# The planner of a diffusion step's instruction order keeps account of which engine last used each PSUM bank

## The chip, the cores and the metric

The kernel runs on one core of one Trainium2 chip. The time is the device time of one execution in microseconds; of several runs the median is given. Five engines work side by side, each through its own queue in order: TensorE (PE, with its weight loads shown as PEld), VectorE (DVE), ScalarE (ACT), GpSimd (POOL) and SyncE (SP), whose queue issues the DMAs. TensorE writes its products into PSUM, which DVE and ACT read; PSUM is used here as eight banks, `bank0` to `bank7`, each of 128 partitions by 512 float32 columns (line 492).

## The reference

One inference step of a backbone with two layers over 384 tokens (256 latent tokens, 128 context tokens) of width 1024, all in float32. Cut to what matters:

```
for l in range(2):
    sh1, sc1, gt1, sh2, sc2, gt2 = split(silu(cond) @ w_mod[l] + b_mod[l], 6)   # for each token group
    h = rmsnorm(x, g[l,0]) * (1 + sc1) + sh1
    if l == 0:      # neighbourhood attention and bidirectional retention, 8 heads each
        z = h @ w_in_even;  m = concat(attention(z), retention(z)) @ w_out_even
    else:           # bidirectional HGRN2, 8 heads of 128
        z = h @ w_in_odd;   m = (rmsnorm(scan_fw(z) + scan_bw(z)) * silu(gate)) @ w_out_odd
    x = x + gt1 * rmsnorm(m, g[l,1])
    h = rmsnorm(x, g[l,2]) * (1 + sc2) + sh2
    x = x + gt2 * rmsnorm((silu(h @ w_a) * (h @ w_u)) @ w_o, g[l,3])
```

Returned are the tokens of both groups, the keys and values of the context, and the final states of retention and HGRN2.

## The kernel before

**Tiling.** The tokens lie transposed, as eight tiles of 128 features by 384 tokens (`x`, and `hh`, `hl` for a high and a low part of the normed tokens). Weights come in chunks of eight 128 x 128 blocks: a DMA into `wr`, a rounded copy `wh` by ACT, the rest `wl = wr - wh` by DVE (`split_weights`, line 536; three buffers of each). A block product is then three matmuls of 384 columns: `wh` with `hh`, `wl` with `hh`, `wh` with `hl` (`gemm`, line 649). A gemm holds one bank for each output tile; when the last matmul of a tile is emitted, an eviction is started that reads the bank and gives it back.

**Stages.** Layer 0: input products, attention, retention, output products; norm step; feed-forward (FFN) in and out; norm step. Layer 1: input products, eight HGRN2 mixers, output products; norm step; FFN. The last FFN product has tokens as rows, and its six banks are read by `leave` (line 1047). Beside this the modulation of both layers is computed, partly by TensorE (`mod_pe`, whose result ACT copies to `mev` and TensorE sums, `mod_pe_out`, line 604) and partly by DVE (`mod_dve`, line 622, with the tile `mscr`).

**What sets the order.** The program is written as some dozens of streams, Python generators, each of which yields its instructions one after the other (a tuple is issued as one) or a condition to wait for. A list scheduler, the class `Machine`, has a clock for each engine and a cost for each instruction. For the next instruction of each stream it takes the earliest start: the engine's clock, or what `deps` returns, whichever is later. It emits the one with the least start (in steps of 1/20 us, after an added lateness), and among equal ones the one of the least priority number (lines 195 to 203). `emit` moves the clock on and notes the end. Thus the order on every engine is settled while the program is built; on the chip, semaphores hold each instruction until what it depends on is done. Nothing of the planner's times remains in the program, only its order.

`deps` looks at regions: a reader waits for the last write of an overlapping region, a writer for its last reads and writes. Ends are counted later by `LEAVE` (0.20 us for PE, 0.13 for DVE, 0.14 for ACT) and starts on PE by `ARRIVE` (0.15). A matmul of fp32 operands costs 4 columns / 2400 us a column, times 0.3 where it fills 32 partitions (lines 226 and 227); a DVE operation on 384 columns 0.06 + 384/960 = 0.46 us.

**Places where two engines are in one bank**, with no region in common or both reading:

- The norm step (class `Step`, from line 884). `chain` (line 914) takes four banks. Column sums of squares go into the first, a root follows, and its reciprocal is spread over 128 partitions by matmuls (`unspread`, line 726). `moments` (line 936) does the same for the norm after the update, and the result stands in columns 0 to 383 of `b2`. There DVE reads it for the first two or three feature tiles (`normed`, line 969: `scr<-x,bank`, then ACT writes `hh` and a float32 copy, and DVE forms `hl`); after two tiles ACT copies it to `rB`. All the while `keep_busy` (line 733) has TensorE multiply constants into columns 384 to 511 of `b2`, in groups of four matmuls (`bank<-cb,ca`). `GAPS` (line 84) says how many groups there may be in each stretch; after the last spread it is five. Each of the four matmuls shows as two rows in the profile. `update` (line 961) scales and adds the layer's output to `x`, reading the first spread from a bank too (`ka<-ka,bank` in the first step).
- The eviction before a norm step (`Post.__call__`, line 771): ACT squares the bank into a scratch tile, and then ACT or DVE scales it by the modulation's gate (`fy<-bank,mod` after the first FFN).
- `probabilities` (line 1175): DVE adds biases to the first 384 columns of a bank whose last 128 are written by a later matmul.
- `retention` (line 1234): DVE reads two halves of a bank, then TensorE writes the first half again.
- `mixer` (line 1458): ACT copies the first half of a bank while TensorE transposes into the second; ACT copies 384 columns of another while TensorE writes column sums behind them.
- `leave`: ACT squares a bank, DVE multiplies it. The early norm (`squares`, line 821): ACT takes a root of 96 columns, DVE copies them.

Of the kernel before, what the change touches and what calls it, by code (L numbers as in the profile page):

```python
# [65 lines left out]
class Op:  # L66
# [3 lines left out]
    def __init__(self, eng, call, outs, ins, cost, table=None):  # L70
        self.eng, self.call, self.cost, self.table = eng, call, cost, table
        self.outs = [region(a) for a in outs]
        self.ins = [region(a) for a in ins]
# [37 lines left out]
class Machine:  # L111
    def __init__(self):
        self.clock = {"PE": 0.0, "DVE": 0.0, "ACT": 0.0, "POOL": 0.0, "SP": 0.0, "DMA": 2.8}
        self.mem = {}
        self.streams = []
        self.table = None

    def spawn(self, gen, prio, late=0.0, margin=0.0):
        self.streams.append(Stream(gen, prio, late, margin))

    def deps(self, op):
        t = 0.0
        for name, a, b, lo, hi in op.ins:
            for r in self.mem.get(name, ()):
                if r[0] < b and a < r[1] and r[2] < hi and lo < r[3] and r[4] > t:
                    t = r[4]
        for name, a, b, lo, hi in op.outs:
            for r in self.mem.get(name, ()):
                if r[0] < b and a < r[1] and r[2] < hi and lo < r[3]:
                    if r[4] > t and op.eng != "PE":  # L130
                        t = r[4]
                    if r[5] > t:
                        t = r[5]
        return t + ARRIVE[op.eng]

    def emit(self, op):
        c = self.clock
        t = max(c[op.eng], self.deps(op))
        if op.eng == "SP":
            c["SP"] = t + 0.07  # L140
            end = c["DMA"] = max(t + 1.5, c["DMA"]) + op.cost
        else:
            cost = op.cost
            if op.table is not None and op.table != self.table:
                self.table = op.table
                cost += 1.3
            if op.eng == "PE" and t < COLD:
                cost *= 2
            end = c[op.eng] = t + cost
        end += LEAVE[op.eng]  # L150
        for name, a, b, lo, hi in op.ins:
            rs = self.mem.setdefault(name, [])
            for r in rs:
                if r[0] == a and r[1] == b and r[2] == lo and r[3] == hi:
                    r[5] = max(r[5], end)
                    break
            else:
                rs.append([a, b, lo, hi, 0.0, end])
        for name, a, b, lo, hi in op.outs:
            rs = self.mem.setdefault(name, [])  # L160
            rs[:] = [r for r in rs if not (a <= r[0] and r[1] <= b and lo <= r[2] and r[3] <= hi)]
            rs.append([a, b, lo, hi, end, 0.0])
        op.call()
# [1612 lines left out]
```

## Time and profile before

| | |
|---|---|
| time, median of 3 runs | 1123.94 us (1121.73 to 1124.01) |
| the profiled execution | 1121.99 us |
| its span, first to last instruction | 1120.2 us |
| PE busy | 1087.0 us (97%), 7048 matmuls |
| DVE busy | 807.5 us (72%), 1491 instructions |
| ACT busy | 556.5 us (50%), 1046 instructions |
| POOL busy | 130.9 us (12%) |
| mean granted TensorE clock | 0.993 |

Names in the profile are `out<-in` by the program's tiles, without buffer numbers, so every bank is `bank`. A line number is often that of a helper (L228 a matmul, L246 an ACT operation, L254 a DVE operation on two tensors), so the tiles tell more than the lines. In rows in order of time the columns are start, duration, engine, line, operation, tiles, shapes, count, and in brackets the engine's idle time before it and what ended that. Matmuls overlap and their ends are modelled, so a busy PE is not a PE at its best; the count of matmuls in a stretch tells more.

### The profile page before, as it was taken

The page shows a single profiled execution, that of the slowest core. Times are in us where ns is not written, and L with a number is a line of the kernel's source. Part 1 is how long each engine was busy: PE and PEld are TensorE (multiplying, and loading weights), DVE is VectorE, ACT ScalarE, POOL GpSimd, SP SyncE. Part 2 cuts the span into 40 slices and gives each one's busy share as a digit, 9 for nine tenths or more (in the row PEclk, how much of TensorE's full clock was granted, in tenths as well). Part 3 has the DMA queues.
Part 4 walks back from the last instruction along what each step waited for, and adds up shares of the span by engine and source line. Part 5 has one row for each costly group of instructions (what it writes and reads, how often), then busy time and mean ns, then how long its engine had stood idle before and what let it go on. Part 6 is the DMA issues. An engine that isn't in the chain of part 4 may idle for free.

```text
span 1120.2 us, 18271 instructions
## 1 busy us (share of the span) xinstructions
PE 1087.0 (97%) x7048; PEld 995.5 (89%) x7048; DVE 807.5 (72%) x1491; ACT 556.5 (50%) x1046; POOL 130.9 (12%) x139
## 2 busy tenths in 40 slices
PE   7999999999999999999999999999999999999997
PEld 5778877989999999989877988889989999998885
DVE  2599986688999998994888589996785434443234
ACT  4587654667333333323765456665676333333322
POOL 1220000000000000333015145442000000000000
PEclk9999999999999999999999999999999999999999
DMA  9966553246666767564442322222324433333331
GB/s 352 364 218 233 183 195 107 94 151 235 243 236 227 245 242 244 208 229 147 150 143 81 109 86 85 86 72 100 109 81 132 151 132 119 127 123 130 115 135 60
DMA packets 51766, 181.48 MB, mean 162 GB/s; under 512 B 8640, under 2 KB 14784, under 8 KB 45152
## 3 DMA queue, kind: packets, MB, share of 16 engines
q1 hardware_dynamic: 51616, 180.24, 45.9%
q8 instruction: 55, 0.90, 0.4%
q14 instruction: 31, 0.25, 0.1%
q0 software_dynamic: 64, 0.08, 0.0%
HBM read 175.83 MB, written 3.42 MB: 160 GB/s over the span
## 4 chain that ended last, share of the span: by engine, by line
PE 75%; DVE 14%; ACT 4%; issue 3%; DMA 3%; POOL 1%; SPq 0%; DVEq 0%; ACTq 0%; POOLq 0%
PE bank L228 74%; DVE wl L254 3%; DVE mscr L267 2%; ACT scr L246 1%; DMA gd<-mod 1%; DVE XB L254 1%; PE bank L232 1%; DVE XA L254 1%; ACT hh L246 1%; DMA mraw<-in_w_mod 1%; POOL ZW L252 1%; DVE scr L260 1%; DMA wr<-in_w_ffn_in 1%; DVE scr L254 0%; DVE T L260 0%
## 5 line engine op out<-in xcount | busy, mean ns | idle before, releaser
L228 PE MATMUL bank<-hh,wh 128*128 128x384 f32 (+1 forms) x1248 | 429.5, 344 | 0.0
L228 PE MATMUL bank<-hh,wl 128*128 128x384 f32 (+1 forms) x1248 | 424.9, 340 | 0.8 <-DVE wl L254 0.8
L228 PE MATMUL bank<-hl,wh 128*128 128x384 f32 (+1 forms) x1248 | 393.1, 345 | 0.0
L254 DVE TENSOR_TENSOR wl<-wr,wh 128x1024 fp32r<-128x1024 f32 x216 | 273.2, 1266 | 156.3 <-ACT wh L246 156.1
L246 ACT ACTIVATE wh<-wr 128x1024 fp32r<-128x1024 f32 x216 | 228.2, 1057 | 167.4 <-PE bank L228 113.8
L228 PEld LDWEIGHTS bank<-hh,wh 128*128 128x128 f32 x1248 | 237.4, 190 | 6.7 <-ACT scr L246 2.4
L228 PEld LDWEIGHTS bank<-hl,wh 128*128 128x128 f32 x1248 | 232.9, 189 | 6.2 <-issue 2.2
L228 PEld LDWEIGHTS bank<-hh,wl 128*128 128x128 f32 x1248 | 237.0, 190 | 1.3 <-DVE wl L254 1.1
L267 DVE SCALAR_TENSOR_TENSOR mscr<-mraw,msb 128x1024 bf16<-128x1024 f32 x128 | 161.1, 1258 | 3.1 <-ACT msb L246 2.0
L246 ACT ACTIVATE fs<-bank 128x384 f32<-128x384 f32 x44 | 21.0, 492 | 90.2 <-PE bank L228 90.2
L228 PE MATMUL bank<-gh,wl 128*128 128x384 f32 x176 | 59.3, 337 | 2.3 <-DVE wl L254 2.2
L228 PE MATMUL bank<-gh,wh 128*128 128x384 f32 x176 | 58.8, 334 | 0.0
L228 PE MATMUL bank<-gl,wh 128*128 128x384 f32 x176 | 58.8, 334 | 0.0
L254 DVE TENSOR_TENSOR fs<-bank,fs 128x384 f32<-128x384 f32 x44 | 24.0, 557 | 40.0 <-PE bank L228 39.8
L228 PE MATMUL bank<-wl,gh 128*128 128x512 f32 x132 | 51.5, 390 | 0.8 <-DVE wl L254 0.8
L228 PE MATMUL bank<-wh,gh 128*128 128x512 f32 x132 | 52.0, 394 | 0.0
L228 PE MATMUL bank<-wh,gl 128*128 128x512 f32 x132 | 51.4, 389 | 0.0
L246 ACT ACTIVATE gh<-fs 128x384 fp32r<-128x384 f32 x44 | 22.3, 519 | 56.1 <-DVE fs L254 56.1
L252 POOL TENSOR_TENSOR rB<-x,fy 128x384 f32<-128x384 f32 x1 | 1.0, 1017 | 382.9 <-DVE mod L254 382.9
L228 PE MATMUL bank<-wh,hh 128*128 128x512 f32 x96 | 40.9, 426 | 0.4 <-DVE wb L271 0.3
L228 PE MATMUL bank<-wh,hl 128*128 128x512 f32 x96 | 38.9, 405 | 2.2 <-DVE hl L254 2.2
L252 POOL TENSOR_TENSOR ZW<-XB,TA 128x192 f32<-128x192 f32 x48 | 36.1, 773 | 32.2 <-ACT XA L246 18.6
(265 smaller groups left out, 1453.8 us busy)
## 6 DMA issues: line engine op xcount, KB each, us to landing
mraw<-in_w_mod SPq DMA_DIRECT2D x48, 1024.0 KB, 5.5
wr<-in_w_ffn_in SPq DMA_DIRECT2D x88, 512.0 KB, 3.3
wr<-in_w_ffn_out SPq DMA_DIRECT2D x44, 512.0 KB, 3.3
wr<-in_w_in_odd SPq DMA_DIRECT2D x40, 512.0 KB, 3.2
wr<-in_w_in_even SPq DMA_DIRECT2D x28, 512.0 KB, 5.0
wr<-in_w_out_even SPq DMA_DIRECT2D x8, 512.0 KB, 3.2
wr<-in_w_out_odd SPq DMA_DIRECT2D x8, 512.0 KB, 3.2
bias<-in_bias SPq DMA_DIRECT2D x8, 384.0 KB, 4.2
```

The costliest lines, as they stand in the source:

```text
L228: return Op("PE", lambda: self.nc.tensor.matmul(out, lhsT=lhsT, rhs=rhs, start=start, stop=stop), [out], [lhsT, rhs], cost + 0.004)
L232: return Op("PE", lambda: self.nc.tensor.transpose(out, in_, ident), [out], [in_], 0.11)
L246: return Op("ACT", lambda: self.nc.scalar.activation(out, in_, func, **kw), outs, ins, 0.1 + width(in_) / 1200, table)
L252: return Op("POOL", lambda: self.nc.gpsimd.tensor_tensor(out=out, in0=a, in1=b, op=op), [out], [a, b], 0.12 + n * 0.0021)
L254: return Op("DVE", lambda: self.nc.vector.tensor_tensor(out=out, in0=a, in1=b, op=op), [out], [a, b], 0.06 + n / 960)
L260: return Op("DVE", lambda: self.nc.vector.tensor_scalar(out=out, in0=a, scalar1=s1, scalar2=s2, op0=op0, **kw), [out], ins, 0.19 + width(o ...
L267: return Op("DVE", lambda: self.nc.vector.scalar_tensor_tensor(out=out, in0=a, scalar=s, in1=b, op0=op0, op1=op1, **kw), outs, ins, 0.1 + ...
```

## The change

`Machine` gets a table `bank`: for each tile whose name begins with "bank", the last end of each engine's instructions that read or wrote it. `deps` adds a condition: an instruction that touches such a tile may not start, in the plan, before the other engines' noted ends. Costs, priorities, streams and conditions stay as they were. The instructions are the same; their order on each engine is planned anew.

```
@@ -114,6 +114,7 @@
         self.mem = {}
         self.streams = []
         self.table = None
+        self.bank = {}
 
     def spawn(self, gen, prio, late=0.0, margin=0.0):
         self.streams.append(Stream(gen, prio, late, margin))
@@ -131,6 +132,11 @@
                         t = r[4]
                     if r[5] > t:
                         t = r[5]
+
+        for name, *_ in op.ins + op.outs:
+            for eng, end in self.bank.get(name, {}).items():
+                if eng != op.eng and end > t:
+                    t = end
         return t + ARRIVE[op.eng]
 
     def emit(self, op):
@@ -148,6 +154,9 @@
                 cost *= 2
             end = c[op.eng] = t + cost
         end += LEAVE[op.eng]
+        for name, *_ in op.ins + op.outs:
+            if name.startswith("bank"):
+                self.bank.setdefault(name, {})[op.eng] = end
         for name, a, b, lo, hi in op.ins:
             rs = self.mem.setdefault(name, [])
             for r in rs:
```

More of the change, by code (lines that the diff above doesn't have):

```diff
@@ L116, in __init__ @@
         self.table = None
+        self.bank = {}
     def spawn(self, gen, prio, late=0.0, margin=0.0):
@@ L133, in deps @@
                         t = r[5]
+        for name, *_ in op.ins + op.outs:
+            for eng, end in self.bank.get(name, {}).items():
+                if eng != op.eng and end > t:
+                    t = end
         return t + ARRIVE[op.eng]
@@ L150, in emit @@
         end += LEAVE[op.eng]
+        for name, *_ in op.ins + op.outs:
+            if name.startswith("bank"):
+                self.bank.setdefault(name, {})[op.eng] = end
         for name, a, b, lo, hi in op.ins:
```

## The prediction

> **What bounds the kernel now.** I read the page first, then stretches of time, then the waits, then the order in time at the three norm steps.
>
> ```profile
> span 1120.2 us, 18271 instructions
> PE 1087.0 (97%) x7048; PEld 995.5 (89%) x7048; DVE 807.5 (72%) x1491; ACT 556.5 (50%) x1046; POOL 130.9 (12%) x139
> PE 75%; DVE 14%; ACT 4%; issue 3%; DMA 3%; POOL 1%; SPq 0%; DVEq 0%; ACTq 0%; POOLq 0%
> ```
>
> ```profile
> core 0: us, PE busy (x) PEld busy (x) DVE busy (x) ACT busy (x) POOL busy (x), PEclk, DMA share, GB/s
> 260.00:280.00 20.00, 20.00 (x116) 20.00 (x115) 15.68 (x25) 14.35 (x21) 0.00 (x0) 1.00 0.57 201
> 480.00:500.00 20.00, 17.77 (x100) 16.81 (x99) 19.79 (x30) 5.95 (x8) 6.56 (x5) 1.00 0.63 230
> ```
>
> TensorE bounds it: a saturated stretch holds 116 wide products in 20 us (0.172 us each), and no order makes that shorter. An order can only act where TensorE waits: at the norm steps, in the mixers, and where DVE is full and the weight splits come late (480 to 500 us, 16 products short). In the first norm step the waits on one bank can be read directly:
>
> ```profile
> 240.72 1.13 PE L228 MATMUL bank<-rs,cb 128*128 128x96 f32 x8 [0.55 <-DVE rs L277]
> 241.78 0.65 PE L228 MATMUL bank<-cb,ca 128*32 128x128 f32 x16
> 242.35 1.05 PE L228 MATMUL bank<-ca,mev 128*128 128x2 f32 x8
> 242.49 0.56 DVE L254 TENSOR_TENSOR scr<-x,bank 128x384 f32<-128x384 f32 x1 [0.37 <-PE bank L228]
> 243.08 0.98 ACT L246 ACTIVATE hh<-scr,mod 128x256 fp32r<-128x256 f32 x2 [1.03 <-DVE scr L254]
> 243.34 0.64 PE L228 MATMUL bank<-cb,ca 128*32 128x128 f32 x16
> 244.05 0.55 DVE L254 TENSOR_TENSOR scr<-x,bank 128x384 f32<-128x384 f32 x1 [1.00 <-PE bank L228]
> 244.52 0.55 DVE L254 TENSOR_TENSOR ka<-ka,bank 128x384 f32<-128x384 f32 x1
> 244.66 0.43 PE L228 MATMUL bank<-cb,ca 128*32 128x128 f32 x8 [0.68 <-DVE scr L254]
> 245.01 0.45 PE L228 MATMUL bank<-hh,wh 128*128 128x384 f32 x1
> 247.32 0.30 PEld L228 LDWEIGHTS bank<-hl,wh 128*128 128x128 f32 x2 [0.27 <-DVE hl L254]
> ```
>
> The row at 240.72 spreads 1/rms into columns 0 to 383 of a bank. The `cb,ca` rows are keep_busy: filler products into columns 384 to 511 of the same bank, five groups of eight rows (16, 16, 8). DVE reads the first columns at 242.49 and 244.05. No address is shared, yet DVE waits for the filler (0.37, 1.00 us) and the filler for DVE (0.68). So the program holds a whole bank for one engine at a time, and the old planner did not know it.
>
> **The change, part by part.** No instruction is added or removed. The tiles show as `bank` in the rows, so the test on the name should hit. What changes is a ready time, at the places where two engines meet in one bank without meeting in an address.
>
> *The norm steps (three).* By the planner's own costs (lines 99, 226 and 227) a filler group takes 4 x (128 x 4 / 2400 x 0.3 + 0.004) = 0.27 us, and a result of PE counts from 0.20 after its end. With the spread's end as zero, groups could start at 0, 0.27, 0.54, 0.82 and 1.09. DVE is free for its first read at about 0.44 and for the second at 0.90, and the earlier start is emitted first: two groups, read, two groups, read, one group, which is the 16, 16, 8 of the trace. Under the new rule DVE's read may start only 0.20 after the last filler group emitted, while the next group may start at that group's very end. The group always has the earlier start, and priority counts only between equal times. So I expect all five groups ahead of the first read.
>
> What that costs: two groups took 0.57 us (241.78 to 242.35), so five take 1.43. The `ca,mev` products, which the planner prices at almost nothing, stay between them and took 0.99 (242.35 to 243.34). The last product needs 0.08 to drain (0.65 against 0.57) and DVE started 0.06 later. First read: 241.78 + 1.43 + 0.99 + 0.08 + 0.06 = 244.34, that is 1.85 late. Behind it ACT's `hh` pair moves from 243.08 to 244.93 and ends at 245.91; the first wide product, at 245.01 until now because the fifth group stood before it, starts at about 246.0: 1.0 late. The second read follows at 244.8, no longer in TensorE's way, and the `ka` work of 244.52 fits ahead of the first read. The 0.27 wait for `hl` is covered. I take 0.75 us a step, between 0.5 and 1.0; below nothing would need fewer groups than five, which I see no reason for. Three steps: **+2.25**.
>
> *The TensorE clock.* Before the third step's products the clock falls, with the same filler pattern; in the second it doesn't:
>
> ```profile
> 537.35:540.76 3.41, 2.68 (x30) 2.19 (x30) 2.57 (x8) 3.13 (x7) 0.00 (x0) 1.00 0.99 418
> 827.49:830.90 3.41, 2.74 (x50) 2.05 (x40) 2.04 (x7) 2.41 (x6) 0.00 (x0) 1.00 0.02 5
> 830.90:834.32 3.42, 3.42 (x12) 3.42 (x11) 3.39 (x7) 3.42 (x8) 0.00 (x0) 0.50 0.26 80
> 828.75 0.65 PE L228 MATMUL bank<-cb,ca 128*32 128x128 f32 x16
> 830.06 0.43 PE L228 MATMUL bank<-cb,ca 128*32 128x128 f32 x8 [0.67 <-DVE scr L254]
> 830.42 0.45 PE L228 MATMUL bank<-hh,wh 128*128 128x384 f32 x1
> 831.16 0.52 PE L228 MATMUL bank<-hh,wl 128*128 128x384 f32 x1
> ```
>
> Twelve products in 3.42 us where 0.172 each would be 2.06: 1.4 lost. After the change TensorE's last filler ends near 244.2 and the wide products begin near 246.0: an idle 1.8 us in one piece instead of the 0.68 above. The fall then gets likelier in each step. I take one more such window, **+1.4** (bounds: the present one vanishes, -1.4; all three steps have one, +2.8).
>
> [...]
>
> *Evictions that two engines read.* After a squared copy by ACT, DVE scales the same bank (lines 771 on). The planner thought both could start together:
>
> ```profile
> 446.40 0.48 DVE L260 TENSOR_SCALAR fy<-bank,mod 128x256 f32<-128x256 f32 x1 [1.29 <-ACT acc L246]
> 448.46 2.05 DVE L267 SCALAR_TENSOR_TENSOR mscr<-mraw,msb 128x1024 bf16<-128x1024 f32 x1
> DVE fy L260 <- ACT scr L246: 8.9, 3, 3.4
> PEld bank L228 <- DVE wl L254: 3.6, 4, 2.0
> ```
>
> Now the hole may be filled with other DVE work. The 1.29 lies where DVE is full and TensorE later waits 3.6 for `wl`; the 8.9 come later, in stretches where DVE is not the bound. Filled or not is even: **-0.6** (bounds -3.6, and +3.6 where a long `mscr` is put ahead of a split).
>
> *Retention and mixers.* A second product into a bank that DVE still reads, transposes and column sums behind ACT's copies:
>
> ```profile
> PEld bank L228 <- DVE ro L254: 2.5, 3, 1.9
> PEld bank L228 <- DVE at L254: 1.0, 3, 0.4
> PEld bank L228 <- ACT o L246: 1.5, 4, 0.5
> PEld bank L232 <- ACT XA L246: 1.0, 4, 0.3
> ```
>
> TensorE can put wide products ahead of these. But the planner's new knowledge is one read longer (0.3 to 0.5 us), not the 1.9, which is DVE being late; and part of every wait is the change of product kind. I take **-0.4** for each pair, -0.8 (bounds -6.0 and 0).
>
> *At nothing.* In attention, DVE's first read of the scores waits for three groups of products; this cost DVE 1.8 us:
>
> ```profile
> DVE as L254 <- PE bank L228: 1.8, 3, 1.1
> DVE rsd L271 <- ACT rs L246: 2.7, 1, 2.7
> 1114.00 0.69 DVE L254 TENSOR_TENSOR x<-bank,mraw 128x512 f32<-128x512 f32 x1 [0.69 <-ACT hh L246]
> ```
>
> TensorE has other products meanwhile; without them it is at most -1.8. The early norm's 2.7 is ACT's own square root, which DVE's next step needs anyhow. At the end there is no other work to put in the 0.69, and TensorE's order is written out. But from the early norm on, times in the plan shift, and ties fall otherwise; that has no sign and is in the range. DMA starts follow the splits on SP's queue and move with them.
>
> **Sum:** 2.25 + 1.4 - 0.6 - 0.8 = +2.25, against the profiled execution's 1121.99 (span 1120.2 and 1.8 around it): 1124.2. That execution lies 1.95 under the median 1123.94; the four times known (1121.73, 1123.94, 1124.01, 1121.99) average 1122.9. Set on that average, as a new median would be: **1125.2 us**.
>
> **The rivals.** [...]
>
> *Better order wins (faster).* The place is DVE's queue between 446 and 492 us and retention: splits go ahead of readers that cannot start. Price: all 3.6 of the waits for `wl` and 2.5 of those for `ro` vanish. 2.25 - 6.1 = -3.85: 1119.1. It decides once these gains pass the three steps' 2.25 (and no window is added). For it: DVE idles 1.29 in a full stretch. Against it: the same hole can take a `mscr` of 2.05.
>
> *Worse order in the full stretch.* Exactly that: the splits get later and the 3.6 doubles; with the forecast's other terms 1125.2 + 0.6 + 3.6 = 1129.4.
>
> *Nothing moves.* The names don't match, or the filler stays between the reads: 1122.9. Against it: `bank` in every row.
>
> **How the numbers follow.** Forecast 0.34, clock holds 0.20, better order 0.24, worse order 0.14, nothing 0.08. This kernel's times can tell 0.2%, 2.2 us. Slower: forecast less 0.04 for smaller sizes, plus worse order, 0.44; faster: better order, 0.24; the rest, 0.32, is no change. Own range of the forecast, with steps of 0.5 to 1.0, one or two windows, gains of 0 to 2.8: 1123.0 to 1128.7. Both signs are open, so the full range goes from the better order to the worse one and a little beyond, for ties: 1118.5 to 1131.0.
>
> **What would show it.** Right: one row of 40 `cb,ca` products (cut only by `ca,mev`) before the first `scr<-x,bank` in each step, the two reads back to back, the first wide product about 1 us later after the spread; more windows at 0.50. Wrong: 16, 16, 8 again; the waits for `wl` between 440 and 500 gone, or doubled; a mixer stretch with other product counts per 20 us.

## The result, and the profile after

The changed kernel takes 1136.07 us (median of 4 runs, 1134.55 to 1136.97), the kernel before 1123.74 us in its four runs (1121.73 to 1124.01): a ratio of 1.0102, with a 95% interval of 1.0085 to 1.0119. It is slower by 12.3 us. The profiled execution took 1134.55 us, its span is 1132.7 us, the mean granted clock fell from 0.993 to 0.984. The page's head, the engines' busy time and the chain (helpers' line numbers lie nine higher than before):

```profile
span 1132.7 us, 18244 instructions
PE 1091.3 (96%) x7048; PEld 999.4 (88%) x7048; DVE 806.0 (71%) x1491; ACT 555.2 (49%) x1045; POOL 125.5 (11%) x139
PE 74%; DVE 15%; ACT 4%; DMA 3%; issue 3%; SPq 0%; POOL 0%; DVEq 0%; ACTq 0%; POOLq 0%
```

These lines show only that the same 7048 matmuls took longer. Where the time went is read from the starts of the same instruction in both traces, stage by stage. The table gives the time from one landmark to the next in both profiles; the differences add up to what the spans differ by:

| from one landmark of TensorE to the next | before, us | after, us | added |
|---|---|---|---|
| start to the last spread of step 1 (layer 0 with its products) | 240.72 | 249.12 | +8.40 |
| each last spread to the first wide product, three steps | 4.29, 4.35, 4.29 | 5.34, 5.34, 5.33 | +3.08 |
| first wide product of step 1 to the first product of FFN-out | 189.21 | 187.45 | -1.76 |
| from there to the last spread of step 2 | 100.82 | 101.82 | +1.00 |
| first wide product of step 2 to the last spread of step 3 (mixers) | 286.74 | 287.09 | +0.35 |
| first wide product of step 3 to the last stage (FFN) | 189.13 | 190.73 | +1.60 |
| last stage to the end | 100.62 | 100.47 | -0.15 |
| sum | | | +12.52 |

Part of the first row is work moved, not lost: 32 rows of the modulation's products (`mraw,sc`) stood in the first FFN stretch before (from 252.10 on) and stand ahead of that stretch after, which is 1.76 shorter.

**The norm step** has the order that the prediction gave. In order of time, step 1 after:

```profile
250.19 0.43 PE L237 MATMUL bank<-cb,ca 128*32 128x128 f32 x8
250.54 1.05 PE L237 MATMUL bank<-ca,mev 128*128 128x2 f32 x8
251.53 1.08 PE L237 MATMUL bank<-cb,ca 128*32 128x128 f32 x32
252.84 1.01 DVE L263 TENSOR_TENSOR scr<-x,bank 128x384 f32<-128x384 f32 x2
253.42 0.98 ACT L255 ACTIVATE hh<-scr,mod 128x256 fp32r<-128x256 f32 x2 [2.96 <-DVE scr L263]
254.46 0.69 PE L237 MATMUL bank<-hh,wh 128*128 128x384 f32 x1 [1.86 <-ACT hh L255]
```

All 40 filler rows stand ahead of DVE's first read, cut only by the `ca,mev` products; the two reads follow back to back; TensorE then has nothing for 1.86 us.

**The large loss lies in retention**, where the prediction saw at most gains. Four retention heads (pairs of heads, function `retention`) run beside layer 0's input products, and the output products need all four. The last one, before:

```profile
188.18 1.13 PE L228 MATMUL bank<-qk 64*128 64x256 f32 x8
190.15 0.48 PE L228 MATMUL bank<-qk 64*128 64x128 f32 x2
193.00 0.44 PE L228 MATMUL bank<-hl,wh 128*128 128x384 f32 x1
```

Its scores (`bank<-qk`) come at 188.18, and wide products follow it from 193.00 on. After, TensorE and one row of DVE:

```profile
197.99 1.07 PE L237 MATMUL bank<-mraw,sc 128*32 128x256 f32 x16
199.78 1.05 PE L237 MATMUL bank<-ca,mev 128*128 128x2 f32 x8 [0.72 <-ACT mev L255]
200.76 1.53 PE L237 MATMUL bank<-qk 64*128 64x256 f32 x8
202.73 1.45 PE L237 MATMUL bank<-qk 64*128 64x128 f32 x4 [0.45 <-DVE ro L263]
207.69 0.55 PE L237 MATMUL bank<-scr,cse 128*32 128x96 f32 x8 [1.17 <-ACT scr L255]
210.81 2.90 PE L237 MATMUL bank<-scr,cse 128*128 128x384 f32 x4 [2.58 <-DVE scr L263]
214.22 0.69 PE L237 MATMUL bank<-hh,wh 128*128 128x384 f32 x1 [0.51 <-ACT hh L255]
```

```profile
200.94 0.17 DVE L263 TENSOR_TENSOR mod<-bank,bmod 128x8 f32<-128x8 f32 x1 [0.53 <-PE bank L237]
```

The same scores come at 200.76, right behind products of the modulation (`mraw,sc` and `ca,mev`), and the second of them goes on only when DVE has read the modulation's bank (200.94). Between them and the `hh,wh` of 214.22 there is no product with weights at all: what follows a head (scores, weights, values, norm, `hh`) runs as one chain through three engines while TensorE waits. Stretches of time before and after, then three windows of after (columns as in the prediction's windows):

```profile
200.00:220.00 20.00, 20.00 (x109) 18.93 (x108) 12.43 (x19) 10.68 (x17) 0.00 (x0) 1.00 0.38 132
```

```profile
200.00:220.00 20.00, 15.25 (x60) 10.35 (x60) 7.55 (x18) 3.68 (x6) 0.00 (x0) 0.57 0.25 98
199.54:202.95 3.41, 2.73 (x18) 2.18 (x18) 2.23 (x7) 0.18 (x1) 0.00 (x0) 1.00 0.84 316
202.95:206.36 3.41, 3.37 (x16) 1.84 (x15) 0.97 (x4) 0.00 (x0) 0.00 (x0) 0.50 0.67 274
216.60:220.02 3.42, 3.42 (x10) 2.81 (x10) 0.64 (x2) 0.00 (x0) 0.00 (x0) 0.50 0.00 0
```

In 20 us there are 60 matmuls instead of 109. The 49 missing, at 0.172 us each, would be 8.4 us, the loss up to step 1; but this is an estimate, and that it fits so well is chance, since after was ahead when the stretch began: by the starts of their rows 672 products with weights against 633 at 200 us, then 686 against 732 at 220 us. The granted clock is 0.50 from 202.95 to 220.02, five windows; waits and clock together make it.

Why the head waits can be read in the program. A head needs two banks at once for its scores. The output products of layer 0 hold up to four, the head's result one, the norm behind retention one. The four can't be given back, because half of the output products' inputs come out of that norm, which needs all four heads. In the trace after, the modulation's next products take one too, and long before it is given back. Their rows (first and last start) in the stretch from 155 to 262 us, before and then after:

```profile
L228 PE MATMUL bank<-mraw,sc x64: 379/379/403, 235.2 to 253.7; 128*32 128x256 f32 x64
```

```profile
L237 PE MATMUL bank<-mraw,sc x64: 379/379/403, 172.1 to 248.1; 128*32 128x256 f32 x64
```

Before, this work began at 235.2, in the norm step. After, its first products run at 172.1, the next pair at 197.99, and the bank is free when DVE's read of 200.94 is done: by the program, seven banks of eight are held until then, and two are wanted. That was the theory to be tested. The rivals: that the new order in retention is bad whatever the banks are, that the modulation's work costs the time by itself, and that the loss sits in the filler.

### The profile page after: what moved, and what is told of

Same layout as the page of the kernel before. It is cut to its first block, busy times and chain, and to the rows that moved or that the text cites. A ratio compares the mean times of both kernels' runs of the same rounds, so it can differ in the third digit from the quotient of the medians.

```text
span 1132.7 us, 18244 instructions
## 1 busy us (share of the span) xinstructions
PE 1091.3 (96%) x7048; PEld 999.4 (88%) x7048; DVE 806.0 (71%) x1491; ACT 555.2 (49%) x1045; POOL 125.5 (11%) x139
## 3 DMA queue, kind: packets, MB, share of 16 engines
HBM read 175.83 MB, written 3.42 MB: 158 GB/s over the span
## 4 chain that ended last, share of the span: by engine, by line
PE 74%; DVE 15%; ACT 4%; DMA 3%; issue 3%; SPq 0%; POOL 0%; DVEq 0%; ACTq 0%; POOLq 0%
PE bank L237 73%; DVE wl L263 3%; DVE XB L263 2%; DVE XA L263 1%; DVE mscr L276 1%; DMA gd<-mod 1%; ACT scr L255 1%; ACT hh L255 1%; PE bank L241 1%; DMA mraw<-in_w_mod 1%; DVE scr L263 1%; ACT wh L255 1%; DMA wr<-in_w_ffn_in 1%; DVE scr L269 1%; DVE ZW L263 1%
## 5 line engine op out<-in xcount | busy, mean ns | idle before, releaser
L255 ACT ACTIVATE hh<-scr,mod 128x256 fp32r<-128x256 f32 (+1 forms) x64 | 31.8, 538 | 15.5 <-DVE scr L263 14.8
```

The lines of the kernel that those rows point to most:

```text
L255: return Op("ACT", lambda: self.nc.scalar.activation(out, in_, func, **kw), outs, ins, 0.1 + width(in_) / 1200, table)
```

## The experiments

Each kernel was compared with runs of the kernel before on the same chip. There are three readings for each beside its time: when the first spread of step 1 comes (before 238.04, after 246.39), how long TensorE needs from each step's last spread to its first wide product (before 4.29, 4.35, 4.29; after 5.34, 5.34, 5.33), and where the modulation's products lie.

| kernel | median us | ratio to before, 95% | first spread, step 1 | last spread to wide product |
|---|---|---|---|---|
| e1, account without the filler | 1135.31 | 1.0100 [1.0071, 1.0129] | 248.42 | 5.21, 5.90, 5.84 |
| e2, account for the filler's bank alone | 1129.31 | 1.0043 [1.0017, 1.0070] | 238.81 | 5.17, 5.18, 5.18 |
| e3, modulation later | 1124.07 | 0.9999 [0.9973, 1.0024] | 235.49 | 5.33, 5.34, 5.69 |
| e4, old rule, filler in its own bank | 1124.20 | 0.9993 [0.9962, 1.0025] | 238.06 | 3.41, 3.41, 4.05 |
| e5, output products leave two banks | 1122.93 | 0.9980 [0.9966, 0.9995] | 235.22 | 5.33, 5.34, 5.33 |
| e6, old rule, modulation early | 1127.30 | 1.0018 [1.0006, 1.0030] | 243.17 | 4.29, 4.52, 4.85 |
| e7, account from step 1 on | 1127.34 | 1.0022 [1.0009, 1.0035] | 237.85 | 5.34, 5.33, 5.84 |
| e8, e3 and own bank | 1118.58 | 0.9943 [0.9928, 0.9957] | 234.56 | 4.14, 3.42, 3.41 |
| e9, one cost changed by 0.005 us | 1121.48 | 0.9976 [0.9966, 0.9986] | 235.27 | 5.33, 5.33, 5.34 |
| e10, e5 and own bank | 1112.66 | 0.9896 [0.9878, 0.9915] | 235.42 | 3.41, 3.41, 3.41 |
| e11, e4 again, more runs | 1122.94 | 0.9990 [0.9979, 1.0001] | 236.92 | 3.41, 3.41, 3.41 |
| e12, e10 and the gate read later | 1107.36 | 0.9853 [0.9829, 0.9877] | 235.40 | 3.41, 3.41, 3.41 |

**e1: the filler outside the account.** `deps` and `emit` skip the new account for keep_busy's products.

```
-        for name, *_ in op.ins + op.outs:
+        for name, *_ in (() if op.filler else op.ins + op.outs):
...
```

> The changed kernel, but keep_busy's filler stands outside the account: it asks for no wait and notes none. If the filler put ahead of DVE's reads is what costs the norm steps about 1 us each (9.45 - 8.40, 9.68 - 8.69 and 11.07 - 10.03 us between the second spread and the first wide product), and the clock window at 254 us hangs on it, the groups show as 16, 16, 8 again and the time falls by 3 to 4.5 us against the changed kernel, to 1131.5 to 1133. The 8.3 us before the first norm step stay: the rows at the first spread near 246. If the filler is not what costs there, 1135 to 1137. If the whole loss came from the norm steps, about 1124.

Measured: 1135.31, no better than after. Step 1 in order of time:

```profile
252.22 0.43 PE L238 MATMUL bank<-cb,ca 128*32 128x128 f32 x8
252.57 1.05 PE L238 MATMUL bank<-ca,mev 128*128 128x2 f32 x8
253.56 0.43 PE L238 MATMUL bank<-cb,ca 128*32 128x128 f32 x8
254.05 0.56 DVE L264 TENSOR_TENSOR scr<-x,bank 128x384 f32<-128x384 f32 x1 [1.49 <-PE bank L238]
256.37 0.69 PE L238 MATMUL bank<-hh,wh 128*128 128x384 f32 x1
```

The old grouping (two groups, read, two groups, read, one) is back, but the `ca,mev` products, which the planner prices at almost nothing and which took 0.99 us on the chip, now fall between the first two groups. The first read comes 2.90 after the last spread (254.05 less 251.16), where it was 1.77 before. The gain expected from the grouping is eaten by one more mispriced neighbour; and the loss in retention is all there (248.42), so it has nothing to do with the filler.

**e2: the converse.** The kernel before, with the account kept only for a bank in which filler has been written, until keep_busy ends.

```
+            if op.filler:
+                self.filled.add(name)
+            if name.startswith("bank") and name in self.filled:
+                self.bank.setdefault(name, {})[op.eng] = end
...
```

> The kernel before, with the account kept only for the banks that hold filler, so only the norm steps are planned with it. By the prediction's steps (0.75 us each and one more clock window of 1.4): 1123.7 + 3.65 = 1127.4; with 1.0 us each and no window 1126.7. The attention and retention stages stay as in the kernel before (first spread near 238.0). If the delay is taken back in the feed-forward stages that follow, 1123 to 1125.

Measured: 1129.31, and each step longer by 0.88, 0.83 and 0.89 us (5.17 less 4.29, and so on). The filler part of the change alone costs about 2.6 us in the steps; the clock and the stages behind them bring the profile to +6.15.

**e3: the modulation later.** The kernel after, with the condition that lets the modulation go on moved behind layer 0's output products.

```
-        mods.allow = 10
         yield from gemm_tok(PLAN_E2, ready(0), L0.va, L0.va_in)
...
         yield from gemm(PLAN_OUT, KT, lambda k: k in L0.oh, post, keep=1)
+        mods.allow = 10
```

> The changed kernel, with one line moved: TensorE's modulation products 8 to 11 are let go only after the output products of layer 0 (as it happened in the kernel before), so that they hold no bank during retention. Theory of the bank: the last retention head waits for a bank that these products hold from 172 to 201 us while the output products hold four; then its scores come near 194 rather than 201, the five half-clock windows from 203 to 220 go, and the time falls by 6 to 9 us, to 1127 to 1130. Rival, that DVE's decays or other ties make the head late: at least 1134. Rival, that only the moved modulation products (1.7 us of TensorE) count: 1134 to 1136, as they come back later.

Measured: 1124.07, better than expected. The first spread comes at 235.49: 10.9 earlier than after, and 2.55 earlier than before. So the loss in retention goes with the modulation's early bank. No window of half clock is left between 165 and 490. With that bank out of the way, the new order of layer 0 is, in this profile, a little better than the old one. The steps still cost 5.33 and more.

**e4: a bank for the filler.** The kernel before; `chain` takes a fifth bank and keep_busy writes there and gives it back.

```
-            b, self.b, r1, self.b2 = yield from banks.take(4)
-            M.spawn(keep_busy(self.b2[:, NT:512], lambda: self.r2 is rB), 9)
+            b, self.b, r1, self.b2, fb = yield from banks.take(5)
+            M.spawn(keep_busy(fb[:, NT:512], lambda: self.r2 is rB, fb), 9)
...
```

> The kernel before, in the same order, with the filler in a fifth bank of its own, so that no read waits for it and it waits for none. If the shared bank costs real waits in the kernel before, DVE's second read comes right behind the first (0.5 us rather than 1.56 us later), and the first wide product 0.5 to 0.9 us earlier after the second spread, in three steps: 1121 to 1122.5. If the filler then runs out early and the clock falls in more steps, 1123.5 to 1126. If nothing of it lies on the path, 1123 to 1124.

Measured: the two reads stand back to back, the steps shrink to 3.41, 3.41 and 4.05, by 0.88, 0.94 and 0.24 us; the time can't be told from before. With the filler in another bank the waits of DVE's first two reads for it (0.37 and 1.00 us before) are gone: in step 1 the two reads take 1.01 us together, from 242.07 on.

**e5: one more bank for retention.** The kernel after, with the modulation where it is; the output products must leave two banks free, not one.

```
-        yield from gemm(PLAN_OUT, KT, lambda k: k in L0.oh, post, keep=1)
+        yield from gemm(PLAN_OUT, KT, lambda k: k in L0.oh, post, keep=2)
```

> The kernel after, but layer 0's output products must leave two banks free instead of one when they take a bank, so that they hold at most one bank less. The modulation still takes its bank during retention. Theory (the last retention head waits for its two banks because the modulation holds one and the output products hold four): its scores come about 5 to 9 us earlier than the 203.8 of after, the first spread of step 1 lies at 236 to 239 instead of 246.4, and the whole is 1126 to 1129. Rival (the order in retention is bad in itself, whatever the banks): the first spread stays at 244 to 247 and the time at 1134 to 1137.

Measured: 1122.93, better than expected, and a first spread at 235.22; the modulation still starts at 172.4. The last head's scores no longer wait for the modulation's end:

```profile
190.86 1.07 PE L237 MATMUL bank<-mraw,sc 128*32 128x256 f32 x16
191.86 1.13 PE L237 MATMUL bank<-qk 64*128 64x256 f32 x8
192.93 1.05 PE L237 MATMUL bank<-ca,mev 128*128 128x2 f32 x8
193.91 1.08 PE L237 MATMUL bank<-qk 64*128 64x128 f32 x4
```

They start at 191.86, ahead of `ca,mev`, 8.9 us earlier than after, and the stretch from 200 to 220 us holds 107 matmuls at clock 1.00. This separates the bank from the modulation's work: the same early start, one bank more, and the first spread comes 11.2 us earlier. The rival by which the order itself is bad falls.

**e6: the modulation early under the old rule.** The kernel before, with the priority and lateness that the first eight chunks have given to the next two as well.

```
     def mod_late():
-        if mods.n < 8:
+        if mods.n < 10:
             return 0.0
```

> The kernel before, with no account of banks, but the modulation's two product pairs that were put off until after layer 0's output products get the same priority and lateness as the first eight, so that they move into retention as in after. Theory (it takes the modulation's bank, the four output banks and the late retention head together): the modulation alone moves the scores of the last head by less than 3 us and the whole stays within 1123 to 1128. Rival (the moved modulation alone does it, by its TensorE time and its bank): the first spread of step 1 comes at 244 or later, the whole at 1131 or more.

Measured: 1127.30, ratio 1.0018. The modulation's products start at 169.9, and the last head's scores move by only 0.57 us (their last row; the first by 0.09), as the theory says. But the first spread is 5.13 later, close to what the rival asked for: the modulation's own TensorE time and one window of half clock at 192.95 come ahead of step 1, and 2.97 of the 5.13 are given back before FFN-out, where that work is then missing. So under the old rule early modulation costs something by itself. Under the new one, with banks enough, it doesn't show: e5, with it early, and e3, with it late, reach the first spread within 0.27 us. The 8 us of after need the bank shortage.

**e7: the account from step 1 on.** Layer 0 is planned as before.

```
-            if name.startswith("bank"):
+            if self.account and name.startswith("bank"):
...
         mods.allow = 12
+        M.account = True
```

> The kernel after, with the account of banks kept only from the first norm step on, so that layer 0 up to there has the order of before. Theory (retention lost 8 to 9 us, the three steps 1.0 each, the rest is the clock and the mixers): the first spread of step 1 at 237.5 to 238.5 as before, each step's first wide product 1.0 later behind its last spread, the whole 1126.5 to 1130. Rival (the account costs the later stages too, hidden behind the shift of 8): 1131 or more.

Measured: 1127.34, ratio 1.0022 [1.0009, 1.0035], first spread 237.85, steps longer by 1.05, 0.98 and 1.55. This is the change from step 1 on, without layer 0: slower by 1.0 to 3.9 us.

**e8: late modulation and the filler's own bank**, the edits of e3 and e4 on the kernel after.

> The kernel after, with the modulation's products put off until layer 0's output products are out, as in the run that did only this (1124.1, first spread of step 1 at 235.5), and the filler in a fifth bank of its own. If the two gains add up, each step's first wide product comes 3.4 to 4.1 us after its last spread instead of 5.3 to 5.7, and the whole is 3 to 5 us under that run: 1119 to 1121.5, faster than before. If the clock or the mixers take it back: 1122 to 1125.

Measured: 1118.58, 0.6% faster than before. Beside e3's ratio of 0.9999, the filler's own bank brings 0.6% under the new rule.

**e9: five thousandths of a microsecond.** The kernel after, with one constant of the planner changed.

```
-LEAVE = {"PE": 0.2, "DVE": 0.13, "ACT": 0.14, "POOL": 0.08, "SP": 0.9}
+LEAVE = {"PE": 0.2, "DVE": 0.13, "ACT": 0.135, "POOL": 0.08, "SP": 0.9}
```

> The kernel after with a single cost of the planner changed by a twentieth of a tenth: a result of ACT counts from 0.135 us after its end instead of 0.14. Theory (the loss in retention hangs on one tie, the moment at which the modulation finds a bank free): the modulation's products fall back behind layer 0's output products, the first spread of step 1 lies at 236 to 239 instead of 246.4, each step still costs 1.0, and the whole is 1123 to 1128. Rival (the account always costs retention 8 us): first spread at 244 or later, the whole at 1133 or more.

Measured: 1121.48, ratio 0.9976 [0.9966, 0.9986]. The modulation is back behind the output products:

```profile
L237 PE MATMUL bank<-mraw,sc x64: 379/379/403, 232.7 to 245.3; 128*32 128x256 f32 x64
```

The same account of banks, with a cost changed by 0.005 us, is faster than before, and by the two ratios to before (1.0102 and 0.9976) some 14 us faster than after, although each step still costs 5.33. So the sign of this change hangs on such a detail of the planner's times. That it is the moment at which the modulation finds a bank free fits, but the whole plan shifts with the constant, so e9 alone does not show it.

**e10: one more bank and the filler's own bank**, the edits of e5 and e4 on the kernel after.

> The kernel after with both other remedies: layer 0's output products leave two banks, and the filler has a fifth bank of its own; the modulation stays in retention. If the gains add up as they did with the late modulation, it lies 3 to 5 us under the run with one more bank alone (1122.9): 1118 to 1120, as fast as the run with late modulation and own bank (1118.6). If one remedy takes the other's gain: 1121 to 1124.

Measured: 1112.66, better than expected. Step 1:

```profile
239.21 0.43 PE L237 MATMUL bank<-cb,ca 128*32 128x128 f32 x8
239.48 1.01 DVE L263 TENSOR_TENSOR scr<-x,bank 128x384 f32<-128x384 f32 x2
240.55 1.08 PE L237 MATMUL bank<-cb,ca 128*32 128x128 f32 x32
241.56 0.45 PE L237 MATMUL bank<-hh,wh 128*128 128x384 f32 x1
```

DVE reads while the filler runs. Against before, the profile gains 2.57 up to the last spread of step 1, 2.70 in the three steps, 2.36 in the first FFN stretch, where modulation products stood, 1.19 up to step 2, 3.45 in the mixers, and then loses 4.19 in layer 1's FFN.

**e11: the own bank under the old rule again**, the kernel of e4.

> The kernel before with the filler in a fifth bank, again, with more rounds beside the run above: what the own bank is worth without the account of banks. The three steps were 0.88, 0.94 and 0.24 us shorter, the profile 1.3 us in all: 1122 to 1124 where before is 1124 to 1125. If the account itself gains nothing once the filler is out of its way, the run above comes out the same; if the account gains 2 to 4 us in layer 0 and before step 3, as the last spreads at 821 against 826 of before suggest, the run above is 2 to 5 us faster than this.

Measured: 1122.94, ratio 0.9990 [0.9979, 1.0001]: 10.3 us behind e10 on the same chip. The own bank alone shortened the steps to 3.41, yet the time hardly moved: its profile loses 4.64 in layer 1's FFN, much as e10 does. That loss is not there in every execution: e4's profile, of the same kernel, loses 0.24 there. The account with one bank more (e5, 0.998) and the filler's bank (0.999) bring little alone, and e10, which has both, 1%.

**e12: what takes 4 us back in layer 1's FFN.** In e10 ACT, TensorE and SP's queue show it, in this order:

```profile
854.50 1.06 ACT L255 ACTIVATE wh<-wr 128x1024 fp32r<-128x1024 f32 x1 [9.01 <-DMA wr<-in_w_ffn_in]
855.61 0.69 PE L237 MATMUL bank<-hh,wh 128*128 128x384 f32 x1 [3.21 <-ACT wh L255]
856.87 0.69 PE L237 MATMUL bank<-hh,wl 128*128 128x384 f32 x1 [0.57 <-DVE wl L263]
```

```profile
833.93 1.05 SPq L302 DMA_DIRECT2D gd<-mod  x2
846.41 0.81 SPq L302 DMA_DIRECT2D mraw<-gd  x2
847.32 41.23 SPq L302 DMA_DIRECT2D wr<-in_w_ffn_in  x12
```

SP writes the last gate to memory (`gd<-mod`, function `gate_rows`) and then has to wait for it before it can issue the read back at 846.41; the next weights stand behind that until 847.32. The gate's 4 KB go out in packets of 4 bytes (in the trace before, some 2100 of them between 847 and 850 us), and need long to land (the kernel before, transfers by kind: name, queue, operation, count, KB each, median us to landing):

```profile
wr<-in_w_ffn_in SPq DMA_DIRECT2D x88, 512.0 KB, 3.3
...
gd<-mod SPq DMA_DIRECT2D x2, 4.0 KB, 12.0
```

The edit lets ten weight chunks be used before the read is issued; nothing needs it before the last stage.

```
             yield I.dma(gd[who].rearrange("(t p) -> p t", p=P), mod[1][:, 40:48, who])
+        n = W.used + 10
+        yield lambda: W.used >= n
```

> The kernel with one more bank free and the filler in its own bank (1112.7), in which the two transfers that read the modulation's last gate back from memory are issued ten weight chunks later; every other instruction stays where it was in its engine's order. Theory (the weight transfers of layer 1's FFN stand on SP's queue behind these two, which wait 11 us for the gate to be written; TensorE then waits 3.5 and 1.1 us for one chunk, and its clock falls for 6.8 us): the waits of ACT for in_w_ffn_in near 855 go, TensorE has no piece of idle time over 1 us between 840 and 900, the first product of the last stage comes 3 to 6 us earlier than 1011.5, and the whole is 1107 to 1110. Rival (the chunk is late for the width of the memory path, not for the queue): the waits stay and the whole is within 2 us of 1112.7.

Measured: 1107.36, ratio 0.9853 [0.9829, 0.9877]. SP's queue now, and the window from 845 to 865 us in e10 and then in e12:

```profile
833.93 1.05 SPq L302 DMA_DIRECT2D gd<-mod  x2
837.85 35.19 SPq L302 DMA_DIRECT2D wr<-in_w_ffn_in  x10
873.10 0.90 SPq L302 DMA_DIRECT2D mraw<-gd  x2
```

```profile
845.00:865.00 20.00, 16.22 (x76) 15.50 (x75) 5.19 (x7) 4.72 (x6) 0.00 (x0) 0.83 0.63 211
```

```profile
845.00:865.00 20.00, 20.00 (x116) 20.00 (x115) 9.54 (x12) 7.58 (x11) 0.00 (x0) 1.00 0.56 178
```

116 products instead of 76, and no fall of the clock before 1101 us. The kernel of e12 is 1.5% faster than before and 2.5% faster than after (by the two ratios to before), with the same instructions in other places.

## Why the prediction was wrong

The forecast, 1125.2 us, had the direction and missed the size; the time lies 5 us above the range's upper end. Even the direction was half luck: the steps' loss was forecast, but it is only 3.08 of the 12.52 us, and the largest part comes from a stage that was forecast as a gain. Without layer 0 (e7: 1.0 to 3.9 us slower) the forecast's +2.25 would have been about right.

**The norm steps: right in mechanism, 0.83 too small.** Order, cause and place came as forecast. The working arrived at 1.0 us a step and then took 0.75; measured were 1.05, 0.99 and 1.04, so 3.08 in place of 2.25. The first read came 1.95 later after its spread (3.72 against 1.77) where 1.85 was worked out. e2 confirms it from the other side (0.88, 0.83, 0.89 alone), e4 shows that the shared bank costs real waits. Shading a number that the rows gave, with no row for the shading, was the mistake.

**The clock: one window more at the steps, as forecast, and partly by luck.** After step 1 there is a new window of half clock at 254.15, step 2 has none, step 3 keeps its one (841.24). But such windows come and go: e9, with the same 5.33 a step, has none at any step, and of e4 and e11, one kernel, only e4 has one at step 3 (827.52). That a longer idle piece makes a fall likelier was the author's estimate and is not shown: after, TensorE idles 1.86, 1.85 and 1.85 us ahead of the first wide products of the three steps, and the clock fell at the first and the third alone. What the term did not have are the five windows in retention (where before had two, at 165.3) and one at 499.91. In the window before the fall at 202.95 TensorE was busy for 2.73 of 3.41 us.

**Evictions: small, but no gain.** DVE's 1.29 us of idle time behind the first squared copy became 0.16, and `mscr` and splits were put ahead of it. But the hole only moved on: before the next eviction (465.52) DVE now waits 1.30, where it had not waited:

```profile
454.08 0.74 DVE L269 TENSOR_SCALAR fy<-bank,mod 128x256 f32<-128x256 f32 x2 [0.16 <-ACT acc L255]
465.52 0.74 DVE L269 TENSOR_SCALAR fy<-bank,mod 128x256 f32<-128x256 f32 x2 [1.30 <-ACT scr L255]
```

TensorE's waits for `wl` between 440 and 505 us went from 3.6 to 3.2, and the stage from FFN-out to step 2 took 1.00 longer, with a window of half clock at 499.91 in it, where -0.6 was forecast. The rival of a worse order there (3.6 doubled) is refuted, and so is the one in which these waits all vanish.

**Retention and mixers: this step failed.** The term was -0.4 each, "bounds -6.0 and 0". The reasoning looked at waits and asked which of them the new knowledge could fill. (The change of product kind that it counted into every wait shows before where the weight loads wait for no other engine: they idle 0.25 us at 187.88, 0.33 at 189.24, 0.24 at 191.77, 0.17 at 193.00.) It did not ask who else might take a bank in the new plan. The part up to step 1 grew by 8.40 (with the modulation's moved products in it); e3 and e5 take that away by two different edits, each of which leaves the last head its two banks; the mixers cost 0.35. The upper bound of zero had no reason behind it.

**"Times in the plan shift, and ties fall otherwise; that has no sign and is in the range": this sentence carried the result.** It was true that it has no sign: e9 moves the whole by some 14 us with 0.005 us in one constant. It was not in the range, because its size was never worked out from a row. It could have been bounded: a head's chain of scores, weights, values and norm without cover takes from 200.76 to 214.22 in the trace after, and in the trace before the heads hold the same chain, covered by wide products, from 188.18 on. Which of the streams shares a scarce resource with it (eight banks, four and two and one of them spoken for) stands in the program.

**Better order wins:** this rival came true in layer 0, though not in the run of the change itself. With the bank freed, the first spread comes 2.5 to 2.8 us earlier than before (e3, e5, e9), and e5 and e9 are faster than before in spite of the dearer steps. The waits for `wl`, which I took for most of its price, did not bring it (3.2 after); where exactly the 2.5 us come from was not traced.

**DMA starts follow the splits:** not worked out, and dearer than thought. In the trace before, SP's queue waits 182 times for `wl`, 704.2 us in all. A wait of TensorE for one chunk of weights in layer 1's FFN comes and goes (in the profiles that stage lost 4.2 us in e10, 4.6 in e11, 1.6 of after's 12.5, but 0.2 in e4 and 0.3 in e8), and e12, which moved the transfer that held up SP's queue, is 2.9 shorter there than before. So some of after's loss in that stage may belong to the execution and not to the order.

What stays open: which instruction of the plan first made the free bank visible to the modulation at 172. The plans differ from the early norm on, and only the end of that chain was tested. Also that the mixers' share went from +0.35 (after) to -3.45 (e10) is not traced to a single wait.

## What to carry to other kernels

A change in a list scheduler's model is a change of every order, and its largest effect may lie where the model did not matter: look for the resource that the streams take for long (banks, buffers), count who holds it when the longest chain wants it, and vary a cost by a few thousandths of a microsecond (here one such variation was run) to see how much of a result is luck. Give filler work a bank that nobody reads, and then tell the scheduler about banks: neither alone brought more than some 0.2%, both with enough banks for the chain brought 1%. And do not issue, ahead of weights on their queue, a transfer that must still wait for another (before, SP's queue stood 11.1 us for the gate).

## What the runs showed of the hardware

The granted clock fell to 0.50 for 3.41 us (from 830.90, before), for 6.83 (from 165.30, before) and for 17.07 (from 202.95 to 220.02, after). It stayed there after the first 3.41 us of the last although TensorE was busy, by its rows, for 3.37 of them: 16 matmuls did not bring it back. Nor did the busy share ahead of it decide its fall: in the trace before it fell after a window with 2.74 us busy (827.49) and not after one with 2.68 (537.35). Eight `ca,mev` products of two columns took 0.99 us (250.54 to 251.53), 0.12 each, where a wide product of 384 columns takes 0.172, so a planner that prices by columns misses them. And 4 KB written in packets of 4 bytes took 12.0 us to land, where weight chunks of 512 KB took 3.3.
